# A second queue for part of the conditioning weights in the output stage of a hybrid decoder block

## The chip, the cores and the metric

The kernel runs on one core of one Trainium2 chip. A core has a matrix engine (TensorE, PE in the profile), a vector engine (VectorE, DVE), a scalar engine (ScalarE, ACT), a general engine (GpSimd, POOL) and SyncE (SP), which here only issues transfers. Each engine executes its own instruction stream in order and waits on semaphores for the others. Transfers between the chip's main memory and the core's on-chip memory (SBUF) go through 16 DMA engines that all queues share; the profile calls the queue fed by SP "hardware_dynamic" (q1) and the queue fed by POOL "software_dynamic" (q0). The metric is the device time of one execution in microseconds (us).

## The reference

One block of a decoder, for 256 prompt tokens and 8 x 4 sampled tokens, with D = 2048, all in float32. What matters here, cut from the reference:

```
mod = silu(c) @ w_ada + b_ada
sh1, sc1, g1, sh2, sc2, g2 = split(mod, 6, axis=-1)
h   = rmsnorm(x, norm1) * (1 + sc1) + sh1
proj = h @ w_in                          # pooling mixer, SSD mixer
...
mix = concatenate([pool_out, ssd_out], -1) @ w_out
x   = x + g1 * mix                       # the output stage
h2  = rmsnorm(x, norm2) * (1 + sc2) + sh2
ffn_out, new_ffn = conv_ffn(h2, st_ffn, w_up, ffn_conv_w, ffn_conv_b, w_down)
x   = x + g2 * ffn_out
```

The six parts of `mod` are the conditioning. Part 4 (`sc2`, the scale of the second norm) is a 2048 x 2048 slice of `w_ada`; nothing needs it before `h2`.

## The kernel before, in words

**Layout.** Activations are kept transposed, channels on the 128 partitions and the 288 tokens (256 + 32) along the free axis. A projection with 2048 inputs is 16 k-tiles; `mm3` makes each 128 x 128 weight tile into three matmuls, with the weight split into a rounded part `whi` and a remainder `wlo`, and the operand into `bh` and `bl`.

**Weights.** `load` (L276) takes a tile of 128 x 1024 floats (512 KB) from a ring of buffers and issues one transfer for it on SP (L279). `split_steps` makes `whi` by a cast on ACT (L298) and `wlo` by a subtraction on DVE (L300). In the output stage the raw tiles of weights come from a ring of 8 buffers, `whi` and `wlo` from rings of 4, and the conditioning's raw tiles (tag `rawa`) from a ring of 13, which is `RAWA + RAW2 + RAW3[1]` = 4 + 4 + 5.

**The output stage** (`for m in range(16)`, from L1212). One step m makes 128 channels of `mix @ w_out` from two halves of weights, `raw_out_m_0` and `raw_out_m_1` (8 k-tiles each), with 48 matmuls of `out_units`, which go to two accumulators: `mm_out` for the SSD mixer's tiles and `mm_outp` for the pooling mixer's. `out_norm` then scales `mm_out` (DVE, `oz`, L1179); `residual` adds gate times result to x: prompt tokens on DVE (`x`, L1169), sampled tokens as a product on DVE (`rs`, L1172) and an addition on POOL (`x`, L1175), once for `mm_out` and once for `mm_outp`. `squares` makes x squared on ACT (`sqa`, L1185) and adds it to a running sum on POOL (`rt`, L1189).

**The conditioning beside it.** `ada_visits((4,), AO, apart=True)` is a generator that is advanced 0.42 of a step (`pull(adas, VA[2])`) after each group of matmuls. It loads part 4 in 32 chunks `raw_adap_4_k_h` (k = 0 to 15, h = 0 or 1; 512 KB each) and multiplies them on PE in four visits of eight chunks (`whole`, L414, 32 matmuls a visit), the last chunk first: visit 0 uses chunks 3_1 down to 0_0, visit 1 chunks 7_1 down to 4_0, and so on. The first 13 chunks find the ring empty. From the fourteenth on (6_1) each chunk reuses the buffer of one thirteen places earlier, so its load waits until the visit that used that buffer has multiplied it: 6_1 to 9_0 wait for visit 0, and so on.

**The order.** The program is written by a scheduler that puts instructions in order on each engine from priorities and estimated times; the split's two instructions have high priority. At run time each engine keeps to that order, and only waits decide when an instruction starts. After the stage come `upk` (the first weights of the up projection, eight halves), and `fill_in` (L1242), which multiplies the first chunks of part 5 while the second norm is finished.

Of the kernel before, what the change touches and what calls it, by code (L numbers as in the profile page):

```python
# [18 lines left out]
P = 128  # L19
# [20 lines left out]
RAW0, RAW1, RAWA, RAW2 = 8, 4, 4, 4  # L40
RAW3 = 4, 5
# [13 lines left out]
AK, AO = 2, 4  # L55
# [28 lines left out]
def _xbc_chunks(bi):  # L84
    (k0, gk), (a, b) = BLOCKS[bi]
    mper = RAWC // (gk * P)
    cuts = [a, *([4, 8] if bi == 0 else []), *range(a + (12 if bi == 0 else mper), b, mper), b]
    return [(list(range(k0, k0 + gk)), list(range(m, n))) for m, n in zip(cuts, cuts[1:])]
# [35 lines left out]
def _halves(nk):  # L124
    return [(0, 8), (8, nk - 8)]
# [41 lines left out]
def kernel(ctx: ExitStack, tc, ins, outs):  # L167
    nc = tc.nc
    S = _STREAM
    wflat = ins["wflat"]  # L170
# [102 lines left out]

    wp = [None]

    def load(key, ring="raw"):  # L276
        off, cols = S.items[key]
        t = wp[0].tile([P, RAWC], F32, tag=ring, name="raw_" + "_".join(map(str, key)))
        nc.sync.dma_start(t[:, :cols], wflat[off:off + P * cols].rearrange("(p n) -> p n", p=P))  # L279
        return t  # L280

    queue = deque(_need_order())
    ahead = {}
    nloads = [0]

    def top_up():

        while queue and nloads[0] - min((n for n, _ in ahead.values()), default=nloads[0]) < RAW0 + RAW1 + RAWA:
            key = queue.popleft()
            ahead[key] = (nloads[0], load(key))  # L290
            nloads[0] += 1
# [4 lines left out]
    def split_steps(raw, a, n, name):  # L296
        hi = wp[0].tile([P, RAWC], F32R, tag="whi", name="whi_" + name)
        yield nc.scalar.copy(hi[:, :n], raw[:, a:a + n])  # L298
        lo = wp[0].tile([P, RAWC], F32R, tag="wlo", name="wlo_" + name)
        yield hi, lo, nc.vector.tensor_tensor(lo[:, :n], raw[:, a:a + n], hi[:, :n].bitcast(F32), ALU.subtract)  # L300
# [17 lines left out]
    def project_units(key, nk, opnd=None, order=None):  # L318

        name = "_".join(map(str, key))  # L320
        ps = pm.tile([P, 512], F32, tag="mm", name="mm_" + name)
        for h, (k0, n) in enumerate(_halves(nk)):
            hi, lo = ready.pop(key + (h,), None) or split(load(key + (h,)), 0, n * P, f"{name}_{h}")
            for i in range(n):
                k = k0 + i
                ko = order[k] if order else k
                bh, bl = (xhi[0][ko], xlo[0][ko]) if opnd is None else opnd(k)
                mm3(ps[:, :N], hi, lo, i, bh, bl, k == 0, k == nk - 1)
                if k % YK == YK - 1 or k == nk - 1:
                    yield ps  # L330
# [7 lines left out]
    def ada_sb(ps, nb, name, r=P):  # L338
        asb = kp.tile([P, 512], F32, tag="asb", name="asb_" + name)
        nc.scalar.copy(asb[0:r, :nb], ps[0:r, :nb])  # L340
        return asb
# [13 lines left out]
    def ada_group_units(gi):  # L355
# [8 lines left out]
        for q0 in range(0, nq, AQ[gi]):  # L364
            raws = [(q, fetch(("ada", gi, q)) if gi else load(("ada", gi, q)))
                    for q in range(q0, min(q0 + AQ[gi], nq))]

            order = [(q, raw, kk) for q, raw in (raws[::-1] if gi else raws) for kk in range(0, per, kstep)]
            for n, (q, raw, kk) in enumerate(order):
                if gi == 0 and kk == 0:  # L370
                    yield
                k = q * per + kk
                for j in range(nj if gk > 1 else 4):
                    if gk == 1:

                        ck, c = k + j // 2, kk * 256 + j * P
                    else:
                        ck, c = k, kk * nj * nb + j * nb
                    begun = gi > 0 and n + j > 0
                    with tc.high_priority() if begun else nullcontext():  # L380
                        i = nc.tensor.matmul(ps[32 * j:32 * j + 32, :nb], sc_c[:, ck, :], raw[:, c:c + nb],  # L381
                                             start=q0 + n == 0, stop=q0 + AQ[gi] >= nq and n + 1 == len(order),
                                             tile_position=(0, 32 * j))
                    if begun:
                        tc.keep_in_program_order(i)
            if gi and q0 + AQ[gi] < nq:
                yield
# [20 lines left out]
    def whole(ps, chunks, step, pin, begun=0):  # L408

        n = 0  # L410
        for k, h, raw in chunks[::-1]:
            for j in (2 * h, 2 * h + 1):
                with tc.high_priority() if n else nullcontext():
                    i = nc.tensor.matmul(ps[32 * j:32 * j + 32, :], sc_c[:, k, :],  # L414
                                         raw[:, 512 * (j % 2):512 * (j % 2) + 512], start=not begun and k == step - 1,
                                         stop=k == KT - step, tile_position=(0, 32 * j))
                if n or pin:
                    tc.keep_in_program_order(i)
                n += 1

    def ada_visits(parts, step, ps=None, begun=0, apart=False):

        plan = [(part, k0) for part in parts for k0 in range(begun, KT, step)]
        ahead, end = [], None

        def chunks(v):
            part, k0 = plan[v]
            for k in range(k0, k0 + step):
                for h in range(2):
                    ahead.append((k, h, load(("adap", part, k, h), "rawa")))  # L430
                    if apart:
                        yield
            for _ in range(1 if apart else 3):
                yield

        yield from chunks(0)
        for v, (part, k0) in enumerate(plan):
            if end:
                ada_end(*end)
                end = None  # L440
            if k0 == 0:
                ps = pa.tile([P, 512], F32, tag="ada", name=f"adap{part}")
            whole(ps, ahead, step, True, begun)
            ahead.clear()
            if k0 + step == KT:
                end = part, ada_sb(ps, 512, f"p{part}")
            yield
            if v + 1 < len(plan):
                yield from chunks(v + 1)
        ada_end(*end)  # L450
        yield

    def ada_end(part, asb):
        pt = ada_tr(asb, 512, f"p{part}")
        with tc.high_priority():
            nc.vector.tensor_tensor(ada[:, part].rearrange("p (j i) c -> p i j c", j=4),
                                    pt.rearrange("p (i j c) -> p i j c", i=4, j=4)[:, :, :, 0:NC9],
                                    bada[:, part].rearrange("p (j i) -> p i j", j=4).unsqueeze(3)
                                    .to_broadcast([P, 4, 4, NC9]), ALU.add)
        if part == 4:  # L460
            ada_scale(1, 4, vec[:, V_N2:V_N2 + KT], 0, KT)
# [76 lines left out]
    for q in range(4):  # L538
        t = mx.tile([P, 4, N], F32, tag="blk", name=f"xa{q}", bufs=4)
# [416 lines left out]
    def chain(*gens):  # L956
        for gn in gens:
            yield from gn

    adas = ada_visits((2, 3), AK)  # L960
    with in_order(*(e.engine for e in (nc.tensor, nc.scalar, nc.vector))):
        nc.scalar.activation(warm, sc_c[:, 0, 0:1], AF.Sqrt, scale=0.0)
        warm_pe(WU[0])
        ssum = aux("ssum1")
        for q in range(4):
# [5 lines left out]
            for i in range(4):  # L971
# [18 lines left out]
        parts = [split_steps(t, 0, len(ms) * P, f"xbc0_{i}") for i, (t, (_, ms)) in  # L990
                 enumerate(zip(first, _xbc_chunks(0)))]
# [55 lines left out]
    for bi in range(len(BLOCKS)):  # L1047
        last = bi + 1 == len(BLOCKS)
        top_up()
        if last:  # L1050
# [6 lines left out]
            raw = load(("dt",))[:, :KT * NH].rearrange("p (k h) -> p k h", h=NH)  # L1057
# [6 lines left out]
            ps = pm.tile([P, 512], F32, tag="mm", name="mm_dt")  # L1064
# [26 lines left out]
    n = 0  # L1091
# [13 lines left out]
            next(late[m])  # L1105
    drain(adas)
    wp[0].move("rawa", "rawa", "raw")
    adas = ada_visits((4,), AO, apart=True)
    for h, (_, n) in enumerate(_halves(KT)):
        ready[("out", 0, h)] = split(load(("out", 0, h)), 0, n * P, f"out_0_{h}")  # L1110
    drain(back)
# [11 lines left out]
    for g in range(4):  # L1123
        for t in range(3):
            k = 4 + 3 * g + t
# [125 lines left out]
    with in_order(nc.tensor.engine, nc.scalar.engine, nc.vector.engine):  # L1251
# [8 lines left out]
        for k in (0, 0, 1, 0, 1):  # L1260
            next(mod[k], None)
        rstd2 = rstd2()
        drain(mod[1])
        ready[("upk", 2)] = upk(2)
    adag2 = ada_visits((5,), AO, ps5, GA, True)
    up0 = [(pm.tile([P, 512], F32, tag="mm", name=f"mm_up{i}") if i < 3 else aux(f"mm_up{i}"))
           for i in range(2 * FK)]
# [131 lines left out]
    with in_order(nc.sync.engine, nc.scalar.engine, nc.vector.engine):  # L1399
        for i, (m0, n, own) in enumerate(YC):  # L1400
            v = x[:, m0:m0 + n, :]
            eng, r = (nc.gpsimd, rstdf) if own else (nc.vector, rstdp)
# [148 lines left out]
```

## Time and profile before

Three runs took 1345.21, 1345.21 and 1346.83 us, median 1345.21 us. The profile is of one further execution.

| quantity | before |
|---|---|
| profiled execution's own time | 1346.4 us |
| its span, first to last instruction | 1344.6 us |
| granted TensorE clock, mean | 0.998 of full speed |
| PE busy over the span | 1328.4 us, 99% |
| DVE, ACT, POOL busy | 822.8, 580.3, 223.1 us |
| output stage between 391 and 500 us: PE busy | 107.83 of 109 us |
| same stretch, mean DMA rate | 317 GB/s |
| the four visits on PE begin at | 393.65, 417.87, 441.50, 464.31 us |

Times of single instructions are given from the start of the span. PE's matmuls overlap, so that each is listed with 0.29 us while the next one starts 0.13 us after it; a wait shows as a larger step from one start to the next. In a row of the timeline the bracket holds the engine's idle time before the instruction and what ended it. "SPq" and "POOLq" are the queues' issuing instructions.

### The profile page before, as it was taken

The numbers are of one execution on the slowest core, as the hardware profiler recorded it, in microseconds if no ns is written. First come the engines' busy times: TensorE is split into PE (matmuls) and PEld (weight loads), VectorE is DVE, ScalarE is ACT, GpSimd is POOL, SyncE is SP. The second block draws the span as 40 slices with busy tenths as digits, with TensorE's granted clock in tenths as the row PEclk, the third lists the DMA queues.
The fourth block names the chain that finished last, engine by engine and source line by source line (L and its number), as shares of the span: only waits on it lengthen the run. The fifth ranks groups of instructions, "written<-read, shape, count | busy, mean of one in ns | idle before, by whom it ended". The sixth has DMA issues, their size and how long they took to land.

```text
span 1344.6 us, 26157 instructions
## 1 busy us (share of the span) xinstructions
PE 1328.4 (99%) x10523; PEld 1247.1 (93%) x10523; DVE 822.8 (61%) x1375; ACT 580.3 (43%) x913; POOL 223.1 (17%) x449
## 2 busy tenths in 40 slices
PE   9999999999999999999999999999999999999997
PEld 7899988776788889999999999999999999999997
DVE  5776569878754568555565455665655556666543
ACT  5243244677733335433433333434433334443552
POOL 0000012123122222102121001221210011122221
PEclk9999999999999999999999999999999999999999
DMA  9999778888898866687455455555544555555521
GB/s 375 405 370 373 272 266 308 308 318 299 306 402 354 324 237 228 229 311 282 172 201 171 167 179 184 203 185 196 182 162 172 190 190 193 194 190 191 188 69 71
DMA packets 97482, 323.19 MB, mean 240 GB/s; under 512 B 10768, under 2 KB 19920, under 8 KB 97360
## 3 DMA queue, kind: packets, MB, share of 16 engines
q1 hardware_dynamic: 93456, 310.72, 63.0%
q0 software_dynamic: 3184, 9.69, 2.0%
q8 instruction: 82, 1.34, 0.4%
q10 hardware_dynamic: 720, 1.11, 0.2%
q14 instruction: 40, 0.33, 0.1%
HBM read 309.78 MB, written 10.39 MB: 238 GB/s over the span
## 4 chain that ended last, share of the span: by engine, by line
PE 93%; DMA 3%; DVE 2%; ACT 1%; issue 0%; POOL 0%; SPq 0%; DVEq 0%; ACTq 0%; POOLq 0%
PE mm_down L313 7%; PE mm_down L312 7%; PE mm_down L314 7%; PE mm_val L313 6%; PE mm_gate L313 6%; PE mm_gate L312 6%; PE mm_gate L314 6%; PE mm_val L314 6%; PE mm_val L312 6%; PE xbc L312 4%; PE xbc L313 4%; PE xbc L314 4%; PE adap L414 4%; PE adag L381 2%; DMA raw_adap<-wflat 2%; PE mm_out L314 2%
## 5 line engine op out<-in xcount | busy, mean ns | idle before, releaser
L313 PE MATMUL mm_down<-al,whi_down 128*128 128x288 f32 x688 | 202.5, 294 | 0.0
L312 PE MATMUL mm_down<-ah,whi_down 128*128 128x288 f32 x688 | 202.4, 294 | 0.0
L314 PE MATMUL mm_down<-ah,wlo_down 128*128 128x288 f32 x688 | 202.0, 294 | 0.0
L313 PE MATMUL mm_val<-h2l,whi_val 128*128 128x288 f32 x640 | 189.1, 296 | 0.0
L313 PE MATMUL mm_gate<-h2l,whi_gate 128*128 128x288 f32 x640 | 189.1, 295 | 0.0
L314 PE MATMUL mm_val<-h2h,wlo_val 128*128 128x288 f32 x640 | 188.4, 294 | 0.0
L314 PE MATMUL mm_gate<-h2h,wlo_gate 128*128 128x288 f32 x640 | 188.4, 294 | 0.0
L312 PE MATMUL mm_gate<-h2h,whi_gate 128*128 128x288 f32 x640 | 188.3, 294 | 0.0
L312 PE MATMUL mm_val<-h2h,whi_val 128*128 128x288 f32 x640 | 188.0, 294 | 0.0
L300 DVE TENSOR_TENSOR wlo_down<-raw_down,whi_down 128x1024 fp32r<-128x1024 f32 x96 | 109.1, 1137 | 115.4 <-ACT whi_down L298 115.4
L300 DVE TENSOR_TENSOR wlo_gate<-raw_gate,whi_gate 128x1024 fp32r<-128x1024 f32 x80 | 98.9, 1237 | 131.5 <-ACT whi_gate L298 131.5
L298 ACT CAST whi_down<-raw_down 128x1024 fp32r<-128x1024 f32 x96 | 92.3, 962 | 164.7 <-PE mm_down L313 135.3
L298 ACT CAST whi_gate<-raw_gate 128x1024 fp32r<-128x1024 f32 x80 | 84.1, 1051 | 156.6 <-PE mm_gate L313 80.3
L298 ACT CAST whi_val<-raw_val 128x1024 fp32r<-128x1024 f32 x80 | 84.1, 1052 | 129.3 <-issue 110.1
L312 PE MATMUL xbc<-h1h,whi_xbc 128*128 128x288 f32 x448 | 133.1, 300 | 0.8 <-ACT h1h L491 0.7
L313 PE MATMUL xbc<-h1l,whi_xbc 128*128 128x288 f32 x448 | 132.3, 296 | 0.0
L314 PE MATMUL xbc<-h1h,wlo_xbc 128*128 128x288 f32 x448 | 130.1, 295 | 0.0
L312 PEld LDWEIGHTS mm_down<-ah,whi_down 128*128 128x128 f32 x688 | 129.2, 188 | 0.0
L313 PEld LDWEIGHTS mm_down<-al,whi_down 128*128 128x128 f32 x688 | 129.1, 188 | 0.0
L314 PEld LDWEIGHTS mm_down<-ah,wlo_down 128*128 128x128 f32 x688 | 129.0, 188 | 0.0
L312 PEld LDWEIGHTS mm_gate<-h2h,whi_gate 128*128 128x128 f32 x640 | 120.3, 188 | 2.5 <-issue 2.5
L314 PEld LDWEIGHTS mm_gate<-h2h,wlo_gate 128*128 128x128 f32 x640 | 120.5, 188 | 0.0
(337 smaller groups left out, 2978.8 us busy)
## 6 DMA issues: line engine op xcount, KB each, us to landing
raw_adap<-wflat SPq DMA_DIRECT2D x128, 512.0 KB, 6.6
raw_gate<-wflat SPq DMA_DIRECT2D x80, 512.0 KB, 3.5
raw_val<-wflat SPq DMA_DIRECT2D x80, 512.0 KB, 3.5
raw_ada<-wflat SPq DMA_DIRECT2D x64, 512.0 KB, 9.6
raw_xbc<-wflat SPq DMA_DIRECT2D x50, 512.0 KB, 9.8
raw_down<-wflat SPq DMA_DIRECT2D x48, 512.0 KB, 3.4
raw_out<-wflat SPq DMA_DIRECT2D x32, 512.0 KB, 9.7
raw_down<-wflat SPq DMA_DIRECT2D x32, 384.0 KB, 3.5
```

Source lines behind the costliest of these rows:

```text
L298: yield nc.scalar.copy(hi[:, :n], raw[:, a:a + n])
L300: yield hi, lo, nc.vector.tensor_tensor(lo[:, :n], raw[:, a:a + n], hi[:, :n].bitcast(F32), ALU.subtract)
L312: nc.tensor.matmul(ps, whi[:, w], bh, start=first, stop=False)
L313: nc.tensor.matmul(ps, whi[:, w], bl, start=False, stop=False)
L314: nc.tensor.matmul(ps, wlo[:, w], bh, start=False, stop=last)
L381: i = nc.tensor.matmul(ps[32 * j:32 * j + 32, :nb], sc_c[:, ck, :], raw[:, c:c + nb], start=q0 + n == 0, stop=q0 + AQ[gi] >= nq and n + 1 ...
L414: i = nc.tensor.matmul(ps[32 * j:32 * j + 32, :], sc_c[:, k, :], raw[:, 512 * (j % 2):512 * (j % 2) + 512], start=not begun and k == step - 1,
```

## The change

`load` gets an argument for the issuing engine, and `ada_visits` an argument `own`: the first `own` chunks go to SP as before, every later one to GpSimd. The only call that gives it is that for part 4, with `own` equal to the size of the ring, 13. So chunks 0_0 to 6_0 stay on SP, and the other 19, 6_1 to 15_1, which are those that wait for a buffer, are issued by POOL and travel on the software queue. Buffers, sizes and matmuls are the same. From L431 on the new program's lines are numbered two higher.

```
-    def load(key, ring="raw"):
+    def load(key, ring="raw", eng=nc.sync):
         off, cols = S.items[key]
         t = wp[0].tile([P, RAWC], F32, tag=ring, name="raw_" + "_".join(map(str, key)))
-        nc.sync.dma_start(t[:, :cols], wflat[off:off + P * cols].rearrange("(p n) -> p n", p=P))
+        eng.dma_start(t[:, :cols], wflat[off:off + P * cols].rearrange("(p n) -> p n", p=P))
         return t
...
-    def ada_visits(parts, step, ps=None, begun=0, apart=False):
+    def ada_visits(parts, step, ps=None, begun=0, apart=False, own=None):
 
         plan = [(part, k0) for part in parts for k0 in range(begun, KT, step)]
-        ahead, end = [], None
+        ahead, end, done = [], None, [0]
 
         def chunks(v):
             part, k0 = plan[v]
             for k in range(k0, k0 + step):
                 for h in range(2):
-                    ahead.append((k, h, load(("adap", part, k, h), "rawa")))
+                    eng = nc.sync if own is None or done[0] < own else nc.gpsimd
+                    ahead.append((k, h, load(("adap", part, k, h), "rawa", eng)))
+                    done[0] += 1
                     if apart:
                         yield
...
-    adas = ada_visits((4,), AO, apart=True)
+    adas = ada_visits((4,), AO, apart=True, own=RAWA + RAW2 + RAW3[1])
```

The scheduler answers with other orders on the engines. On SP, in the output stage around visit 0 (`raw_out_m_h` are halves of the stage's weights, `raw_adap_4_k_h` chunks of the conditioning; lines with - are gone from the place):

```order
 L279 DMA raw_out_5_1_5108<-wflat 128x1024
-L279 DMA raw_adap_4_6_1_5138<-wflat 128x1024
 L279 DMA raw_out_6_0_5155<-wflat 128x1024
-L279 DMA raw_adap_4_7_0_5167<-wflat 128x1024
-L279 DMA raw_adap_4_7_1_5181<-wflat 128x1024
 L279 DMA raw_out_6_1_5189<-wflat 128x1024
 L279 DMA raw_out_7_0_5250<-wflat 128x1024
-L279 DMA raw_adap_4_8_0_5274<-wflat 128x1024
 L279 DMA raw_out_7_1_5282<-wflat 128x1024
-L279 DMA raw_adap_4_8_1_5294<-wflat 128x1024
-L279 DMA raw_adap_4_9_0_5314<-wflat 128x1024
 L279 DMA raw_out_8_0_5331<-wflat 128x1024
```

The stage's halves now follow one another on SP with no chunk of conditioning between them.

On POOL at the same place, before (`rs2_m` is the sampled tokens' product of step m, `rt2` the running sum of squares):

```order
L1175 TENSOR_TENSOR x_4715<-x_4715,rs2_3_4951 128x32
L1175 TENSOR_TENSOR x_4715<-x_4715,rs2_3_4984 128x32
L1189 TENSOR_TENSOR rt2_4716<-rt2_4716,sqa_3_4987 128x288
L1175 TENSOR_TENSOR x_4715<-x_4715,rs2_4_5047 128x32
L1175 TENSOR_TENSOR x_4715<-x_4715,rs2_4_5065 128x32
L1189 TENSOR_TENSOR rt2_4716<-rt2_4716,sqa_4_5068 128x288
```

and on POOL now:

```order
L1177 TENSOR_TENSOR x_4715<-x_4715,rs2_3_4951 128x32
L279 DMA raw_adap_4_8_1_5294<-wflat 128x1024
L1177 TENSOR_TENSOR x_4715<-x_4715,rs2_3_4984 128x32
L279 DMA raw_adap_4_9_0_5314<-wflat 128x1024
L1191 TENSOR_TENSOR rt2_4716<-rt2_4716,sqa_3_4987 128x288
L279 DMA raw_adap_4_6_1_5138<-wflat 128x1024
L279 DMA raw_adap_4_7_0_5167<-wflat 128x1024
L279 DMA raw_adap_4_7_1_5181<-wflat 128x1024
L279 DMA raw_adap_4_8_0_5274<-wflat 128x1024
L1177 TENSOR_TENSOR x_4715<-x_4715,rs2_4_5047 128x32
L279 DMA raw_adap_4_9_1_5349<-wflat 128x1024
L1177 TENSOR_TENSOR x_4715<-x_4715,rs2_4_5065 128x32
```

Six issues now stand between the additions and the sum of step 3 and the first addition of step 4; chunk 7_1, which visit 1 multiplies first, is the fifth of them, and each waits for its buffer. 9_1 and 10_0, which belong to later visits, stand between and behind the additions of step 4. Two similar groups follow: 13_0 and 13_1 between step 6's additions, then 10_1 to 12_1, and later 15_0, 15_1 and 14_1.

On ACT, steps 3 to 6, before (`sqa_m` are the squares of step m, `whi_out_m_h` the cast of a half):

```order
L1185 ACTIVATE sqa_3_4987<-x_4715 128x288
L298 CAST whi_out_5_0_5076<-raw_out_5_0_5074 128x1024
L1185 ACTIVATE sqa_4_5068<-x_4715 128x288
L298 CAST whi_out_5_1_5110<-raw_out_5_1_5108 128x1024
L298 CAST whi_out_6_0_5157<-raw_out_6_0_5155 128x1024
L1185 ACTIVATE sqa_5_5150<-x_4715 128x288
L298 CAST whi_out_6_1_5191<-raw_out_6_1_5189 128x1024
L298 CAST whi_out_7_0_5252<-raw_out_7_0_5250 128x1024
L298 CAST whi_out_7_1_5284<-raw_out_7_1_5282 128x1024
L1185 ACTIVATE sqa_6_5245<-x_4715 128x288
```

and now:

```order
L1187 ACTIVATE sqa_3_4987<-x_4715 128x288
L298 CAST whi_out_5_0_5076<-raw_out_5_0_5074 128x1024
L298 CAST whi_out_5_1_5110<-raw_out_5_1_5108 128x1024
L1187 ACTIVATE sqa_4_5068<-x_4715 128x288
L298 CAST whi_out_6_0_5157<-raw_out_6_0_5155 128x1024
L298 CAST whi_out_6_1_5191<-raw_out_6_1_5189 128x1024
L298 CAST whi_out_7_0_5252<-raw_out_7_0_5250 128x1024
L298 CAST whi_out_7_1_5284<-raw_out_7_1_5282 128x1024
L298 CAST whi_out_8_0_5333<-raw_out_8_0_5331 128x1024
L1187 ACTIVATE sqa_5_5150<-x_4715 128x288
```

The cast of 5_1 has moved ahead of the squares of step 4, and those of 6_1, 7_0, 7_1 and 8_0 ahead of the squares of step 5. DVE's subtractions `wlo_out` move forward with them; on PE the four visits keep their places among the stage's matmuls. Behind the stage, SP issues five of part 5's chunks (1_0, 1_1, 0_0, 0_1, 2_0) earlier than before, and 5_1, 3_1, 2_1 and 3_0, which wait for visit 3, behind the half `raw_upk_4` and not ahead of `raw_upk_2`.

## The prediction

> **What bounds the kernel now.** I read the page first, then a table of stretches through the output stage, then PE's instructions in the stretches that were not full, and from there the waits backwards: DVE, ACT, SP. The page:
>
> ```profile
> span 1344.6 us, 26157 instructions
> PE 1328.4 (99%) x10523; PEld 1247.1 (93%) x10523; DVE 822.8 (61%) x1375; ACT 580.3 (43%) x913; POOL 223.1 (17%) x449
> ```
>
> PE bounds the whole; a change to queues can win only where PE waits, and lose wherever it makes PE wait. Stretches of the output stage (columns: PE, PEld, DVE, ACT, POOL busy, granted clock, DMA share, GB/s):
>
> ```profile
> 400.00:410.00 10.00, 9.82 (x74) 9.59 (x73) 3.70 (x8) 2.33 (x3) 1.32 (x3) 1.00 1.03 409
> 410.00:420.00 10.00, 9.55 (x77) 7.47 (x79) 6.94 (x13) 3.51 (x5) 2.66 (x5) 1.00 0.69 275
> ```
>
> The clock is full, the DMA engines are saturated in the first and not in the second, and PE has holes in both. PE's own rows at the holes:
>
> ```profile
> 407.04 0.29 PE L312 MATMUL mm_outp<-mixh,whi_out 128*128 128x288 f32 x1
> 407.51 0.40 PE L314 MATMUL mm_out<-mixh,wlo_out 128*128 128x288 f32 x1 [0.18 <-DVE wlo_out L300]
> 407.75 0.29 PE L312 MATMUL mm_out<-mixh,whi_out 128*128 128x288 f32 x1
> ...
> 414.20 0.29 PE L313 MATMUL mm_outp<-mixl,whi_out 128*128 128x288 f32 x1
> 414.95 0.40 PE L314 MATMUL mm_out<-mixh,wlo_out 128*128 128x288 f32 x1 [0.45 <-DVE wlo_out L300]
> 415.19 0.29 PE L312 MATMUL mm_out<-mixh,whi_out 128*128 128x288 f32 x1
> ...
> 437.84 0.29 PE L313 MATMUL mm_outp<-mixl,whi_out 128*128 128x288 f32 x1
> 438.58 0.40 PE L314 MATMUL mm_out<-mixh,wlo_out 128*128 128x288 f32 x1 [0.45 <-DVE wlo_out L300]
> 438.82 0.29 PE L312 MATMUL mm_out<-mixh,whi_out 128*128 128x288 f32 x1
> ```
>
> The usual step is 0.13 us (415.19 less 414.95 is already a slow 0.24). Beyond it, each hole costs its step and a slow restart: 0.34 + 0.11 = 0.45, 0.62 + 0.11 = 0.73, 0.61 + 0.11 = 0.72. Together 1.90 us. All three wait for the remainder of a second half (5_1, 6_1, 9_1), and the brackets understate them, since matmuls overlap.
>
> Why the remainder is late stands on ACT and DVE (engine, then idle before and its releaser):
>
> ```profile
> 397.31 1.05 ACT L298 CAST whi_out<-raw_out 128x1024 fp32r<-128x1024 f32 x1 [1.32 <-PE adap L414]
> 404.82 0.44 ACT L1185 ACTIVATE sqa<-x 128x288 f32<-128x288 f32 x1 [6.46 <-POOL x L1175]
> 405.17 1.98 ACT L298 CAST whi_out<-raw_out 128x1024 fp32r<-128x1024 f32 x2
> 412.25 0.45 ACT L1185 ACTIVATE sqa<-x 128x288 f32<-128x288 f32 x1 [5.10 <-POOL x L1175]
> ...
> 394.19 1.21 DVE L300 TENSOR_TENSOR wlo_out<-raw_out,whi_out 128x1024 fp32r<-128x1024 f32 x1
> 406.24 1.22 DVE L300 TENSOR_TENSOR wlo_out<-raw_out,whi_out 128x1024 fp32r<-128x1024 f32 x1 [1.85 <-ACT whi_out L298]
> ```
>
> ACT stood 6.46 us at the squares of step 4, and the cast of 5_1 (405.17) stood behind them in order; the remainder followed at 406.24 and PE at 407.51. The half itself was long there, as SP's issues and the transfers show:
>
> ```profile
> 390.70 0.33 SPq L279 DMA_DIRECT2D raw_out<-wflat  x1
> 396.39 0.33 SPq L279 DMA_DIRECT2D raw_adap<-wflat  x1
> ...
> 408.79 0.33 SPq L279 DMA_DIRECT2D raw_out<-wflat  x1
> 419.78 0.33 SPq L279 DMA_DIRECT2D raw_adap<-wflat  x1
> ...
> DMA packets 1791, 6.54 MB, mean 409 GB/s; under 512 B 197, under 2 KB 197, under 8 KB 1790
> ...
> raw_out<-wflat SPq DMA_DIRECT2D x6, 512.0 KB, 10.1
> ```
>
> 5_1 was issued at 390.70 and lands 10.1 us later, 400.8. Behind it SP stood 5.4 us (390.99 to 396.39) at chunk 6_1, which waited for visit 0, and 10.6 us at the next visit; 6_0 was queued behind. At 409 GB/s a tile of 512 KB (524,288 bytes) takes 1.28 us of all engines.
>
> **The change, part by part.**
>
> *19 issues leave SP.* SP issues 6_0 right behind 5_1, near 392, and no longer stands in a chunk's wait. An issue on SP is 0.33 us; SP bounds nothing, so this by itself is worth nothing. What it makes possible is the new order.
>
> *The casts move ahead of the squares.* The cast of 5_1 no longer follows the squares of step 4, nor do 6_1 to 8_0 follow those of step 5. If 5_1 lands by 403 (400.8, or two microseconds later if the software queue takes half the engines from about 399), its remainder is done at 403 + 1.05 + 1.22 = 405.3, before PE's 407.2. Half 6_0 comes 2.56 us after it at half rate and is done at 407.8; PE needs it half a step after 407.5, near 410.3. 6_1 follows at 410.4, needed near 413.5. All three are in time: the holes at 407, 415 and 438 close, 1.90 us. The squares themselves then run later, by one cast or a few, and only the sum on POOL waits for them, until the norm at the stage's end; nothing is due earlier. Of two further slow restarts beside these (some 0.3 us by the same reckoning) I count none.
>
> *19 issues come to POOL.* Its rows, and the visits:
>
> ```profile
> 365.22 0.56 POOL L1115 DMA_DIRECT2D o_pool<-npl  x1 [0.30 <-POOL npl L1114]
> 394.42 1.10 POOL L1175 TENSOR_TENSOR x<-x,rs 128x32 f32<-128x32 f32 x1 [0.64 <-DVE rs L1172]
> 403.38 0.25 POOL L1175 TENSOR_TENSOR x<-x,rs 128x32 f32<-128x32 f32 x1 [6.51 <-DVE rs L1172]
> ...
> 393.65 3.57 PE adap L414 x32
> 417.87 3.57 PE adap L414 x32
> ```
>
> An issue costs POOL 0.56 us, 19 of them 10.6 us, of an engine with 1.32 and 2.66 busy in 10. The addition of 1.10 against 0.25 us ran beside DVE's subtraction of 394.19, so DVE can hold POOL for up to its 1.22 us; five issues each held once would be 6 us late at worst, none at best. I take the 0.56, since POOL has 6.51 us of idle behind them. Queued behind 8_1's wait is the second addition of step 3 and its squares; 8_1 waits for the first matmuls of visit 0, near 394, when that addition came at 394.42. A delay of 0.8 us there holds the squares of step 3, and the cast of 5_0 behind them, which waited for PE until 397.31 anyway: it costs nothing. Behind 6_1 to 8_0 (visit 0's end, 397.2) the next work of POOL is at 403.38: hidden too.
>
> *The chunks travel on the software queue.* This is the unknown. What the trace has of that queue beside SP's and without it (landing time last, then two stretches of two microseconds):
>
> ```profile
> o_conv<-ncv POOLq DMA_DIRECT2D x4, 67.5 KB, 6.3
> o_ssms<-hst POOLq DMA_DIRECT2D x16, 384.0 KB, 3.5
> ...
> q1 hardware_dynamic: 409, 0.61, 81.1%
> q0 software_dynamic: 57, 0.18, 22.2%
> ...
> q0 software_dynamic: 109, 0.45, 67.9%
> q1 hardware_dynamic: 49, 0.16, 22.1%
> ```
>
> Where both were at work it moved 0.18 of 0.79 MB (23%) with SP's queue full, and 0.45 of 0.61 MB (74%) with SP's nearly empty. 8_1, first in POOL's order, is issued by 395.2; with the 6.3 us of the small transfer it begins to land by 401.5. The chunk that visit 1 multiplies first, 7_1, is fifth in that order. At an equal share a tile takes 2.56 us, so 7_1 is there between 401.5 + 4 x 2.56 = 411.7 and 401.5 + 5 x 2.56 = 414.3. PE reaches visit 1 at 417.87 less the 1.4 us saved ahead of it (two holes and the slow restart), 416.5: slack 2.2 to 4.8 us. It holds down to a tile in 3.75 us, a share of 34% (43% by the stricter reckoning). At 74% for POOL the halves are late instead. I take the equal share: the two readings, 23% and 74%, lie about evenly round it, and the first of them held transfers of smaller rows. Later rounds have more room, since by then SP is two steps ahead and its queue no longer full.
>
> On the order in which a DMA engine serves two queues the Trainium skill has a rule (DMA: Bandwidth & Descriptors, section "Queues, rings and completion order"): it takes turns between them, but drains a whole packet of about 9 to 17 descriptors from one ring before it switches. If SP's packets were such and POOL's single descriptors, POOL's share would be about a tenth, an estimate from that page. The stretch with 57 against 409 packets (one to seven) leans that way, that with 109 against 49 the other; neither shows nine to one.
>
> *The end of the stage.* Five chunks of part 5 are issued earlier, and three that `fill_in` needs (3_1, 2_1, 3_0) now stand behind `upk_4`:
>
> ```profile
> 469.28 14.14 SPq L279 DMA_DIRECT2D raw_upk<-wflat  x8
> ...
> 491.93 1.85 PE adap L1242 x16
> ```
>
> Issued by about 475, and landing 10.1 us later, 485, they are in time for 491.93 by 7 us; cost 0.
>
> The sum against the profiled execution: 1346.4 - 1.9 = 1344.5 (span 1342.7). The median of the runs shown stands 1.2 lower, at 1345.21, so the forecast is 1345.2 - 1.9 = 1343.3 us.
>
> **Rivals.**
>
> *B, the software queue starves and visit 1 waits: slower.* At the 23% of the first stretch a tile takes 1.28 / 0.23 = 5.6 us and 7_1 lands at 401.5 + 4 x 5.6 = 423.9, 7.4 us after PE wants it; PE would stand there and everything after it be that much later: 7.4 - 1.9 = +5.5, 1350.7 us. It decides from a share of 34% downwards. For it speaks that SP, freed of its waits, has a full backlog exactly then; against it the 74% row. A harsher form: POOL gets a tenth until SP's backlog is gone. SP may be some 12 halves ahead of PE (8 raw, 4 split), and has with those consumed meanwhile 16 to move from 399, until 419.5; then the last 3 to 4 chunks follow, 7_1 near 425: 425 - 416.5 - 1.9 = +6.6, 1351.8 us. That harsher form is what the Trainium skill's rule above would make of it.
>
> *C, the software queue takes the greater share.* With 74% for POOL, what is left of 5_1 at 399.2 (1.6 us of transfer) takes 6.2 us, to 405.4, its remainder ready at 407.7; 6_0 needs 4.9 us more, is ready at 412.6, 2 us late. Some 2.5 us lost against 1.9 saved: 1345.8 us. For it the last two rows, against it that there SP had almost nothing queued.
>
> *D, nothing is won.* The casts come no earlier than before because the halves land late or the split's buffers are the wait, and PE's holes only move: 1345.2 us. For it: the ring of four splits lets a cast start only when PE is done with the half four before, as at 397.31.
>
> **How the numbers follow.** Forecast A 0.50, B 0.27 (0.07 of it the harsher form), C 0.06, D 0.17. A measurement of this kernel can tell about 0.2%, 2.7 us, from no change: its runs differ by 1.6 us. A lies within that unless the slow restarts close too and the runs' step falls well: of its 0.50 I give 0.18 to faster, 0.32 to the same. D goes to the same, C to it with 0.04 and to slower with 0.02; B is slower. That is 0.18, 0.53, 0.29. For the range, A alone would be 1342 to 1344.5; it must take in C and D and some of B until 2 in 10 are left out: 1342.0 to 1350.8.
>
> **What would show it.** In the profile after: 6_0 issued near 392 and SP's wait of 5 us gone; the cast of 5_1 within a microsecond of its landing, ahead of the squares of step 4; no PE step over 0.3 us at the three holes; 7_1 landing at 411 to 414 on the software queue with about half of the packets. Wrong it is if PE's row at visit 1 carries an idle bracket, released by a DMA, of several microseconds, or if POOL's issues take far more than 0.6 us each beside DVE's subtractions.

## The result and the profile after

The changed kernel takes 1343.4 us (median of 21 runs, 1342.69 to 1345.05), the kernel before, run beside it, 1345.68 us (21 runs, 1345.1 to 1346.83). The ratio is 0.9983, 95% interval 0.9976 to 0.9989: 2.3 us less, between 1.5 and 3.2. The profiled execution took 1345.05 us, the slowest of the 21, with a span of 1343.2.

The two queues of the changed kernel in the stretch from 400 to 414 us, from the view of the transfers (packets, MB, share of 16 engines; then the issues of that stretch with KB and median time to landing):

```profile
DMA packets 1573, 5.72 MB, mean 409 GB/s; under 512 B 182, under 2 KB 182, under 8 KB 1572
...
q1 hardware_dynamic: 791, 2.89, 51.8%
q0 software_dynamic: 781, 2.82, 50.6%
...
raw_out<-wflat SPq DMA_DIRECT2D x5, 512.0 KB, 16.0
```

The total rate is the 409 GB/s of before, and the queues halve it, packet for packet: 791 against 781. A half issued by SP now takes 16.0 us to land, against 10.1.

SP and POOL of the changed kernel (timeline):

```profile
390.50 10.53 SPq L279 DMA_DIRECT2D raw_out<-wflat  x7
...
394.79 0.57 POOL L279 DMA_DIRECT2D raw_adap<-wflat  x1 [1.17 <-DMA raw_out<-wflat]
395.37 0.39 POOL L1177 TENSOR_TENSOR x<-x,rs 128x32 f32<-128x32 f32 x1
397.07 2.17 POOL L279 DMA_DIRECT2D raw_adap<-wflat  x4
```

SP issues seven halves in a row from 390.50 and stands nowhere for a chunk. POOL's issues take 0.54 to 0.58 us each.

ACT, the casts of 5_0, 5_1 and 6_0 and the squares of step 4 between them:

```profile
398.66 1.05 ACT L298 CAST whi_out<-raw_out 128x1024 fp32r<-128x1024 f32 x1 [2.42 <-DMA raw_out<-wflat]
405.86 1.05 ACT L298 CAST whi_out<-raw_out 128x1024 fp32r<-128x1024 f32 x1 [6.15 <-DMA raw_out<-wflat]
406.81 0.44 ACT L1187 ACTIVATE sqa<-x 128x288 f32<-128x288 f32 x1
408.42 1.05 ACT L298 CAST whi_out<-raw_out 128x1024 fp32r<-128x1024 f32 x1 [1.17 <-DMA raw_out<-wflat]
```

Each cast now starts within 0.1 us of its half's landing, ahead of the squares, and what ACT waits for is the transfer. On PE two of the three holes of before are gone (PE is busy for all of 10 us in both stretches in which they were), and what is left in this execution is one at 407 (the two stretches, then PE's rows):

```profile
410.00:420.00 10.00, 10.00 (x83) 8.32 (x85) 6.02 (x10) 4.47 (x5) 0.50 (x2) 1.00 1.03 409
430.00:440.00 10.00, 10.00 (x78) 10.00 (x78) 5.83 (x10) 3.94 (x5) 3.26 (x4) 1.00 1.03 408
...
406.49 0.29 PE L314 MATMUL mm_out<-mixh,wlo_out 128*128 128x288 f32 x1
406.96 0.40 PE L312 MATMUL mm_out<-mixh,whi_out 128*128 128x288 f32 x1 [0.18 <-ACT whi_out L298]
407.20 0.29 PE L313 MATMUL mm_out<-mixl,whi_out 128*128 128x288 f32 x1
408.22 0.40 PE L314 MATMUL mm_out<-mixh,wlo_out 128*128 128x288 f32 x1 [0.73 <-DVE wlo_out L300]
```

By the steps from one start to the next (0.47 and 1.02 against 0.13, and two slow restarts) this one costs 1.45 us, three times as much as the hole of before at this place. Half 5_1 landed at 405.8, 15.3 us after its issue. So in this execution the whole stage won only 0.8 us; the repeated profiles below say which of the two readings, 0.8 or 1.9, is the usual one.

### The profile page after: what moved, and what is told of

Its sections match the earlier page's. It is cut to its first block, busy times and chain, and to the rows that moved or that the text cites. A ratio compares the mean times of both kernels' runs of the same rounds, so it can differ in the third digit from the quotient of the medians.

```text
span 1343.2 us, 26179 instructions
## 1 busy us (share of the span) xinstructions
PE 1328.3 (99%) x10523; PEld 1247.7 (93%) x10523; DVE 822.6 (61%) x1375; ACT 581.8 (43%) x913; POOL 234.1 (17%) x468
## 4 chain that ended last, share of the span: by engine, by line
PE 92%; DMA 5%; DVE 2%; ACT 0%; issue 0%; POOL 0%; SPq 0%; DVEq 0%; ACTq 0%; POOLq 0%
PE mm_down L313 7%; PE mm_down L312 7%; PE mm_down L314 7%; PE mm_val L313 6%; PE mm_gate L313 6%; PE mm_gate L312 6%; PE mm_gate L314 6%; PE mm_val L314 6%; PE mm_val L312 6%; PE xbc L312 4%; PE xbc L313 4%; PE xbc L314 4%; PE adap L414 3%; PE adag L381 2%; DMA raw_adap<-wflat 2%; PE mm_out L312 1%
```

## Experiments

For each profile I give, beside the time, PE's excess between 391 and 500 us: what all its steps from one start to the next exceed the usual 0.13 us (0.11 in the conditioning), as a difference to the kernel before. A step that straddles 391 us is counted in; in two profiles, the third of the changed kernel and that of the second queue alone, it makes up 0.3 us. Before 391 the kernels should not differ, but that excess up to 380 us was anything from 59.9 to 62.2 us in the 13 profiles of this study, and between 380 and 391 us anything up to 3.6 us. That is the size of the spread of the runs, so the stretch says more than one span.

**The order alone.** All chunks stay on SP; only the squares move behind the casts.

```
     def squares(m, name):
...
             nc.scalar.activation(sq[:, c], x[:, m, c], AF.Square)
+            mark(f"sq_{m}")
+            if m < KT - 3:
+                behind(f"sq_{m}", f"whi_out_{m + 1}_1")
...
         residual(ps0[1] if m == 0 else pp, 2, m)
-        squares(m, "a")
+        for j in [m - 1] if 0 < m < KT - 2 else [m - 1, m] if m == KT - 2 else [m] if m == KT - 1 else []:
+            squares(j, "a")
```

(`mark` remembers an instruction and `behind` gives the scheduler an order between two instructions of one engine, with no wait.) In the trace of this run SP, POOL and DVE have the order of the kernel before, as far as the names of the tiles tell, and on PE one matmul of the stage has moved.

> The queues of the kernel before (all 32 chunks on SP), but on ACT the squares of each step stand behind the second cast of the next step. Theory 1 (the gain is the casts' place on ACT; the second queue only led the scheduler to it): the holes of PE at 407, 415 and 438 close, 1.9 us, perhaps the one at 386 (0.7 us) too; ratio to before 0.998 to 0.9986. Theory 2 (the gain is SP no longer standing in the chunks' waits): nothing changes, ratio 1.000, since SP stands as long as before.

1343.99 us against 1346.31: ratio 0.9980, interval 0.9971 to 0.9988. The excess between 391 and 500 us fell by 1.97 us, and up to 485 us no step over 0.25 us is left there outside the visits. PE's busy time between 391 and 500 us (107.83 us in the kernel before), then SP and ACT (timeline of this run):

```profile
391.00:500.00 109.00, 108.91 (x838) 93.87 (x837) 61.78 (x117) 36.83 (x53) 24.85 (x42) 1.00 0.84 324
...
390.34 0.33 SPq L279 DMA_DIRECT2D raw_out<-wflat  x1
396.05 0.33 SPq L279 DMA_DIRECT2D raw_adap<-wflat  x1
...
401.18 1.05 ACT L298 CAST whi_out<-raw_out 128x1024 fp32r<-128x1024 f32 x1 [2.80 <-DMA raw_out<-wflat]
405.33 0.45 ACT L1196 ACTIVATE sqa<-x 128x288 f32<-128x288 f32 x1 [3.10 <-POOL x L1186]
```

SP stands 5.4 us in the wait for visit 0 exactly as before, and it costs nothing. The cast of 5_1 starts at 401.18 and not at 405.17, and that is the gain. Theory 2 falls. The hole at 386, which I had thought might close too, stayed at 0.75 us.

**The second queue alone.** The changed kernel with the casts held behind the squares as before.

```
+    PINNED = {"out_5_1": 4, "out_6_0": 4, "out_6_1": 5, "out_7_0": 5, "out_7_1": 5, "out_8_0": 6, "out_8_1": 6,
+              "out_9_0": 7, "out_9_1": 8, "out_10_0": 8}
...
+        mark("whi_" + name)
+        if name in PINNED:
+            behind("whi_" + name, f"sq_{PINNED[name]}")
```

> The queues of the changed kernel (19 chunks on POOL), but the casts of 5_1 to 9_1 and 10_0 are held behind the squares, as the kernel before has them. Theory 1: the holes near 415 and 438 are back, the one at 407 is as large as in the changed kernel; ratio to before 1.000 to 1.001. Theory 2: the time of the changed kernel, ratio 0.9983.

1345.32 against 1346.31 us: ratio 0.9991, interval 0.9982 to 1.0000; excess 0.84 us below that of before, which is 1.0 to 1.2 us above what the changed kernel shows in its other profiles. The order alone, timed with the same runs of the kernel before, has a median 1.3 us lower. The holes are back near 414 and 437, at some two thirds of their size (0.46 us each), and the casts once more follow squares that wait for POOL (ACT, then PE):

```profile
412.03 0.45 ACT L1203 ACTIVATE sqa<-x 128x288 f32<-128x288 f32 x1 [4.37 <-POOL x L1193]
412.38 2.93 ACT L298 CAST whi_out<-raw_out 128x1024 fp32r<-128x1024 f32 x3
...
437.26 0.29 PE L328 MATMUL mm_outp<-mixh,whi_out 128*128 128x288 f32 x1
437.74 0.40 PE L330 MATMUL mm_out<-mixh,wlo_out 128*128 128x288 f32 x1 [0.18 <-DVE wlo_out L304]
```

The expectation of 1.000 to 1.001 was too pessimistic. At 407 there was no hole, although the cast of 5_1 waited for the squares again (405.68): PE's order is not held in this run, and three more matmuls than in the kernel before stand ahead of the first that needs the remainder of 5_1. At 0.13 us each they fill 0.4 us, so that by this reckoning about half of the 0.84 us is PE's order and not the queue. With the queues but without ACT's order more than half of the stage's gain is missing; that all of it is missing is not shown, and by the times alone the interval overlaps that of the changed kernel.

**Eight chunks back on SP.** `own` is 21 and not 13, so that only the chunks that wait for visits 1 and 2 go to POOL.

```
-    adas = ada_visits((4,), AO, apart=True, own=RAWA + RAW2 + RAW3[1])
+    adas = ada_visits((4,), AO, apart=True, own=RAWA + RAW2 + RAW3[1] + 8)
```

> The first 21 chunks on SP, so those that wait for visit 0 too; the 11 that wait for visits 1 and 2 on POOL. The scheduler then leaves the casts of 5_1 and 6_1 behind the squares and moves that of 9_1 ahead of those of step 8. Theory 1: the holes at 407 (0.45 us) and 415 (0.73) stay as before, that at 438 (0.72) goes, no new one comes: 0.7 us less, ratio 0.9995. Theory 2 (each visit's wait on SP costs its hole): about two thirds of the gain, 1.4 us.

1345.76 against 1346.31 us: ratio 0.9993, interval 0.9984 to 1.0002, and an excess 0.82 us below that of before. Hole by hole it is as theory 1 has it (PE at 406 and 413; then the stretch in which the third hole was):

```profile
406.22 0.40 PE L314 MATMUL mm_out<-mixh,wlo_out 128*128 128x288 f32 x1 [0.18 <-DVE wlo_out L300]
413.64 0.40 PE L314 MATMUL mm_out<-mixh,wlo_out 128*128 128x288 f32 x1 [0.46 <-DVE wlo_out L300]
...
430.00:440.00 10.00, 10.00 (x79) 9.42 (x82) 7.63 (x14) 5.17 (x7) 4.00 (x5) 1.00 1.03 408
```

The first two are those of before, 0.47 and 0.76 us from start to start against 0.47 and 0.75; the third is gone, and PE is full from 430 to 440 us. By the runs' times alone theories 1 and 2 are not told apart here.

**No chunks.** The 19 chunks are not loaded; visits 1 to 3 multiply tiles of the first 13 again. The squares stand as in the run with the order alone.

```
-                    ahead.append((k, h, load(("adap", part, k, h), "rawa", eng)))
+                    if own is None or done[0] < own:
+                        held.append(load(("adap", part, k, h), "rawa"))
+                        ahead.append((k, h, held[-1]))
+                    else:
+                        ahead.append((k, h, held[done[0] % own]))
```

> The 19 later chunks are not loaded at all (visits 1 to 3 multiply the first chunks again, so that part 4 of the conditioning is not the reference's); the casts stand ahead of the squares as in the changed kernel. Theory 1 says that the hole of 1.45 us at 407 in the changed kernel comes from the chunks' transfers sharing the DMA engines: half 5_1 lands by 403 instead of 405.8, and PE has no step over 0.3 us at 407; some 1.4 us less than the changed kernel. Rival: SP's own backlog makes 5_1 late, and it still lands after 404.5 with a hole.

The span is 1342.4 us (one execution), the excess 2.19 us below that of before, and up to 485 us PE has no step over 0.25 us outside the visits. Half 5_1, issued at 390.77 and with the same two chunks ahead of it on SP, landed 10.4 us later, at 401.2:

```profile
raw_out<-wflat SPq DMA_DIRECT2D x1, 512.0 KB, 10.4
```

So SP's own backlog does not make it late in this run; in the changed kernel POOL's chunks beside it do. The size expected (1.4 us under the changed kernel) was reckoned from the one profile with the large hole.

**The changed kernel twice more.**

> The changed kernel once more, for its profile. If the hole of 1.45 us at 407 comes from the order of the transfers (SP's backlog and POOL's equal share), half 5_1 lands near 405.8 again (within 1 us) and the hole is there in every execution, so that some 1.4 us of gain are left lying. If it belongs to the one execution profiled (the slowest of 21), 5_1 lands by 404.5 and the hole is under 0.5 us.

> The same once more, to tell a hole that is always there from one that comes and goes: as for the run before it.

Neither has a hole at 407. 5_1 took 13.5 us in the one and landed at 404.1, and landed at 403.8 in the other; their excess is 2.07 and 1.86 us below that of before. A fourth profile, of the timed run below, has 5_1 at 402.8, no hole and 1.81 us. PE's busy time between 391 and 500 us, first of all before:

```profile
391.00:500.00 109.00, 107.83 (x822) 91.97 (x822) 59.42 (x113) 35.71 (x51) 21.07 (x40) 1.00 0.82 317
```

in the first profile of the changed kernel:

```profile
391.00:500.00 109.00, 108.00 (x828) 92.63 (x828) 60.99 (x114) 37.42 (x51) 33.47 (x60) 1.00 0.89 343
```

and in the second:

```profile
391.00:500.00 109.00, 108.83 (x838) 93.85 (x837) 62.34 (x117) 38.41 (x53) 34.15 (x61) 1.00 0.91 347
```

The hole of the first profile is thus of that execution. In the four profiles POOL's first issue came at 394.8, 394.6, 395.6 and 396.9, the software queue's first packet 3.8 us later each time (398.6, 398.4, 399.4 and 400.7), and 5_1 landed at 405.8, 404.1, 403.8 and 402.8: what SP's queue still has to move up to 5_1 at that moment goes at half the rate. In the first profile that was more than in the others, since SP's queue was late before the sharing began. Half 5_0, issued at 386.67, landed 11.9 us later, at 398.6, where the others and the kernel before have 10.3 to 10.9 us:

```profile
raw_out<-wflat SPq DMA_DIRECT2D x1, 512.0 KB, 11.9
```

So two chunks and 5_1, three whole tiles, were still to come, and took 7.2 us. Why SP's queue was late there is open. The second profile closes the hole by little: the remainder of 5_1 was done at 406.48, and PE took it at 406.72. In the third and fourth PE began visit 0 some 0.8 and 2.1 us later than in the first, which gave 5_1 more room. The fourth lost 3.6 us between 380 and 391 us (0.9 in the kernel before).

**POOL's issues ten microseconds later.** In the changed kernel the first group of chunks is held behind the second addition of step 4.

```
+        if eng is nc.gpsimd and key[2] < 11:
+            mark(key)
+            behind(key, "xs_4")
```

> The changed kernel with POOL's chunk issues held behind the second addition of step 4, so near 405 and not 395, with 6_1, 7_0, 7_1 first in order; the cast of 5_1 is behind the squares of step 4 again. Equal share of the engines: 7_1, third, lands 7 us after its issue and two tiles of 2.56 us later, 406 + 7 + 5.1 = 418, PE waits 1 to 2 us at visit 1 (416.5); the hole at 407 is 0.45 us; in all within 1 us of the kernel before. Rival B (the software queue starves behind SP's backlog): 7_1 lands after 421, PE waits over 4 us, 3 us or more slower than before.

1344.7 against 1346.63 us: ratio 0.9989, interval 0.9980 to 0.9998. The first chunk was issued at 405.04, and 7_1, third in this order, landed at 417.2, 12.1 us after that issue. The visit after it:

```profile
416.69 0.29 PE L326 MATMUL mm_outp<-mixh,wlo_out 128*128 128x288 f32 x1
417.22 1.50 PE L426 MATMUL adap<-raw_adap,sc_c 128*32 128x512 f32 x12 [0.23 <-DMA raw_adap<-wflat]
```

That is the edge itself: visit 1 waits 0.3 us for a transfer. The chunks landed 2.56 us apart here too, so the queue did not starve even when it began ten microseconds late; rival B falls. The step at 407 was 0.76 us in this run, as the cast of 5_1 was behind the squares again; with the slow restart it cost 0.74 us and not 0.45. The stage's excess is 1.2 us below that of before, a little more than the 1 us expected at most.

**The order, and DVE at 386.** The order alone, and the remainder of 3_0 ahead of the scaling of step 2 on DVE.

```
+        mark("wlo_" + name)
+        if name == "out_3_0":
+            behind("oz_2", "wlo_out_3_0")
```

> All chunks on SP, squares behind the casts as in the run with the order alone, and on DVE the remainder of 3_0 ahead of the scaling of step 2. If the hole at 386, left in every run so far, is DVE's order (the cast of 3_0 ended 0.6 us before its subtraction began), it shrinks from 0.75 to under 0.3 us and the time falls by a further 0.5 us against the order alone: ratio to before 0.9975 to 0.998. Rival: the half lands too late (384) for that, no further gain.

1344.12 against 1346.63 us: ratio 0.9983, interval 0.9974 to 0.9992, where 0.9975 to 0.998 was expected. The hole is gone; PE's busy time from 380 to 391 us in the run with the order alone:

```profile
380.00:391.00 11.00, 10.54 (x80) 10.31 (x79) 6.45 (x13) 4.28 (x6) 4.86 (x8) 1.00 1.03 410
```

and in this one:

```profile
380.00:391.00 11.00, 11.00 (x86) 11.00 (x85) 6.39 (x13) 4.27 (x6) 3.94 (x8) 1.00 1.03 410
```

By PE's steps this is worth 0.74 us. The times of the two don't show it apart, so the three were timed beside each other.

**Three kernels on one chip.**

> The changed kernel timed beside the two below, on one chip with the same runs of the kernel before. Theory 1 (what is won is won by the order of the casts): 0.998 to 0.9985, and a few tenths of a microsecond more than the two below, since 5_1 lands within a microsecond of its last moment and the hole at 407 opens in some executions.

> The order alone, all chunks on SP. Theory 1: equal to the changed kernel or up to 0.5 us faster. Theory 2 (the second queue adds something of its own): the changed kernel is faster by 0.5 us or more.

> The order with the remainder of 3_0 ahead on DVE. PE's holes in the profile fell by a further 0.74 us against the order alone; if that reaches the end, this is 0.7 us faster than the order alone and the fastest of the three, 0.5 to 1.2 us ahead of the changed kernel.

| kernel (11 runs each; before 1346.16 us, 27 runs) | median, us | ratio to before, 95% interval |
|---|---|---|
| changed kernel | 1343.71 | 0.9983, 0.9974 to 0.9992 |
| order alone | 1344.28 | 0.9986, 0.9977 to 0.9995 |
| order, and DVE at 386 | 1343.97 | 0.9982, 0.9973 to 0.9991 |

The three cannot be told apart: 0.6 us lie between their medians, and each interval is 2.4 us wide. Neither the few tenths that I expected of a hole that opens now and then nor the 0.7 us at 386 can be seen in the times, and nothing here shows that the second queue adds a gain of its own. No version was found that clearly beats the changed kernel.

## Why the prediction was right

The forecast was 1343.3 us, 1.9 less than before; measured are 1343.4, and 2.3 less with an interval that holds 1.9. That the two times lie 0.1 us apart is luck in part: the kernel before took 1345.68 and not the 1345.21 from which I reckoned, and the gain was 0.4 us larger, so that two misses cancel. Going through its steps:

- *The holes are the casts' place behind the squares.* Right, and shown by the order alone: it closes all three holes on its own and gives 0.9980, and 0.9986 when timed again. The queue without the order gives 0.9991, with two holes back.
- *19 issues leave SP; this alone is worth nothing.* Right as far as the runs show: with the order alone SP stands the 5.4 us and PE loses nothing. Of the 0.84 us with the queue alone about half is PE's order; where the rest comes from is open.
- *The sum of 1.90 us.* In the three profiles of the changed kernel without a hole at 407 the stage has 2.07, 1.86 and 1.81 us less excess. In the one taken first it has 0.78.
- *5_1 lands by 403.* This step failed in three profiles of four: 405.8, 404.1, 403.8 and 402.8. I had the half landing at 400.8 without sharing, by the median of other halves; its own row in the kernel before is 10.4 us, so 401.1. And I let the sharing begin at 399 and double the 1.8 us then left. In the first two profiles it began near 398.5: from there 2.6 us of transfer remained to 401.1, which at half rate end at 403.7. The rest goes with SP's queue being late before that, slightly in the second profile (10.9 us for 5_0) and by 1.6 us in the first. The forecast stood by a narrow margin: I had 1.9 us of slack (405.3 against 407.2), and the second profile had 0.2. One execution in four went over; of the two in which PE came to visit 0 no later than in the kernel before, one did.
- *7_1 between 411.7 and 414.3, visit 1 not delayed.* Right in three profiles: it landed at 413.4, 413.2, 414.3 and 415.5, the last where POOL began 2.1 us later. The visit came at 417.7 in the first and was delayed in none. The tiles came 2.5 to 2.7 us apart, as the equal share has it, but for 3.8 to 4.1 us between the third and the fourth, which stays open.
- *POOL's issues at 0.56 us, hidden.* Right (0.54 to 0.58).
- *Part 5's chunks behind `upk_4` cost nothing.* Right: `fill_in` came at 490.99 after and 491.93 before, with the same steps.

Rival B needed a share under 34% and found 50%. Its harsher form drew on the Trainium skill (DMA: Bandwidth & Descriptors, section "Queues, rings and completion order"), by which a DMA engine takes whole packets from two queues in turn. With rows of 4 KB on both queues the trace has 791 against 781 packets, which agrees with taking turns; the size of a turn it does not show. My tenth came from supposing packets of many descriptors on one queue and single ones on the other, and no row here has that. Rival C (74% for POOL) has no row for it either, and rival D's holes did not move elsewhere in three of the four profiles.

## What to carry to other kernels

A wait at the matrix engine that points to a weight's cast may be neither the transfer nor the engine's load, but an instruction with a later need that stands ahead of it in order and waits for a third engine; read what ended the idle time just before the late cast. When a change moves work between queues under a scheduler, hold the two effects apart: pin the old order with the new queues and the new order with the old queues, since the order may be the whole gain; and compare the order on every engine, as a pin on one lets the others move. Here a second queue beside a saturated one added no bandwidth (409 GB/s with it and without) but halved that of the first, so count everything still ahead of the urgent transfer when the sharing begins.

## What I had not expected

The two queues shared the engines almost exactly evenly for as long as both had work (791 and 781 packets in 14 us), with tiles mostly landing 2.56 us apart, twice the 1.28 us of one queue alone. The first chunk of the software queue landed 7.0 us after its issue, of which 3.8 us passed before its first packet. And PE's waits before 380 us differed by 2.3 us over the 13 profiles and by 1.2 us over the four of the changed kernel, with up to 2.7 us more between 380 and 391 us: together as much as the change is worth. A single profile of a change this small can show less than half of it.
